# A two-layer decoder trunk in float32 on one core: both feed-forward stages with twelve up-projection pairs as seven block products each, the weight sums added by GpSimd in SBUF

## The chip, the core and the metric

The kernel runs on one core of a Trainium2 chip. The engines of a core are TensorE (PE in the profile; its weight loads are PEld), VectorE (DVE), ScalarE (ACT), GpSimd (POOL) and SyncE (SP, which issues most DMAs). They have separate instruction queues, each worked in order, and wait for each other by semaphores. The metric is the device time of one execution in microseconds (us), lower is better. The kernel before takes 1279.8 us, the median of 3 runs (1279.74 to 1279.89).

## The reference

Two layers, each a mixer (attention, a convolution module and a short gated convolution over one input projection) and a feed-forward network (FFN), on 16 + 512 = 528 tokens of width 1024. The change concerns the FFN:

```python
D_MODEL, DEPTH, D_FF, FFN_KERNEL = 1024, 2, 2816, 3

def ffn_sublayer(h, pre_g, post_g, w_up, conv_w, w_down):
    u = rms_norm(h, pre_g)
    z = jnp.einsum("bld,df->blf", u, w_up)
    z = causal_depthwise_conv(z, conv_w)
    g, up = jnp.split(z, 2, axis=-1)
    y = jnp.einsum("blf,fd->bld", jax.nn.silu(g) * up, w_down)
    return h + rms_norm(y, post_g)
```

In the last layer only 514 tokens are computed in the up projection and 512 behind it, since the first 16 are dropped.

## The kernel before

**Layout.** Activations lie transposed: 128 partitions are 128 of the 1024 features, the free dimension is the tokens. The 2816 FFN features are 22 chunks of 128. For a chunk f there is a pair of weight chunks, gate (columns 128 f) and up (columns 2816 + 128 f), each 1024 by 128, in SBUF [128, 8 x 128]. The 22 pairs are taken in three parts (`PARTS`: 8, 7 and 7), and after each part its share of the down projection is made and added to `yp`.

**Precision.** Each float32 operand is split into `hi`, rounded to the fast matmul type, and `lo`, the rest. A product is three matmuls: hi·hi, w-hi·u-lo and w-lo·u-hi. For a weight chunk ScalarE makes `whi` (a CAST) and VectorE `wlo` (a subtraction). An ordinary pair is 2 chunks x 8 rows of blocks x 3 x 2 halves of the tokens = 96 matmuls of 264 (layer 0) or 264 and 250 columns (layer 1), in `mm3`.

**Seven products.** In layer 1 only (`SEVEN_IN`), for the twelve pairs in `SEVEN`, the pair is one two-by-two block product: the gate and up chunks, each with an upper and a lower half of the 1024 rows, against two halves of the rows and of the tokens of u. `seven_pair` makes it from seven block products of 4 x 3 = 12 matmuls, 84 in all, of 258 columns, in three PSUM banks x, y and z. The inputs are sums of blocks. Those of u are made once per FFN by `normalised` (tiles t0 to t3, on ScalarE and VectorE, during part 0). Those of the weights, with gate0, gate1, up0, up1 for the halves, are gate0+up0, up0+up1, gate0+up0+up1 and gate0+gate1+up0+up1. A pair has four weight tiles, taken by `next_w` in this order: w (the gate chunk itself), c and b (two sums each) and d (up1 alone). The block sums leave more work to VectorE: 3.5 split chunks instead of 2, and additions behind PSUM.

**Where the sums come from.** `sum_steps` copies halves of the chunks to a DRAM tile `w_sum` with SP's DMAs and adds to them there with three accumulating DMAs of GpSimd's queue. `sums_at` spreads this: eight pairs during the FFN of layer 0, four in the mixer of layer 1. `tick` is a one-column GpSimd copy which ties each step to the progress of the FFN. In layer 1 the sums are loaded like weights.

**Order.** `next_w` keeps two weight tiles ready ahead of the one taken. Within an engine the order is fixed before the launch by a scheduler. `whi`/`wlo` have three buffers, shared by w, c and the down projection; `shi`/`slo` (for b) and the last pair of `y` (for d) have one. Raw weights rotate through three buffers, and in parts 1 and 2 of layer 1 through four more in the tile `h`, which is saved to `h_dram` for that time and loaded again (`spare`, `raw_tile`). `zs` (four buffers) holds up-projection outputs until `ffn_gate` has made the convolution (two SCALAR_TENSOR_TENSOR on VectorE for each of gate and up, behind one ACTIVATE), silu, product and split. In layer 0 the up projection reads the unscaled u, and `scaled` multiplies each output by `rz` on VectorE. `store_one` splits six chunks of layer 1's input projection in advance, in layer 0's down projections, and stores them by GpSimd's DMA (`w_split`).

Of the kernel before, what the change touches and what calls it, by code (L numbers as in the profile page):

```python
# [10 lines left out]
F32 = mybir.dt.float32  # L11
# [5 lines left out]
P = 128  # L17
# [11 lines left out]
PARTS = (8, 7, 7)  # L29


SEVEN = (8, 9, 10, 11, 12, 13, 15, 16, 17, 18, 19, 20)
SEVEN_IN = (1,)
SUMS = {1: (8, 4)}
SUM_US, SUM_LAT, SUM_EVERY = 0.9, 5.0, 40.0
K2 = KD // 2
SB = K2 * P
AHEAD = 2
# [350 lines left out]
def tile_hybrid_trunk(ctx: ExitStack, tc: tile.TileContext, xT, wflat, pv_d, out):  # L389
# [79 lines left out]
    nc.gpsimd.memset(hsel[DH:, DH:], 1.0 / DH)  # L469

    cols = T(const, [P, 4], F32, "cols")
    ticks = cols[:, 3:]
# [41 lines left out]


    up_chunk = {(c[1], c[4][0][0] // P): i for i, c in enumerate(chunks) if c[0] == "ffn_w_up"}
    seven_up = {up_chunk[l, NF + f]: (l, f) for l in SEVEN_IN for f in SEVEN}
    sums = {}

    def flat_w(i):  # L520

        n = chunks[i][3] * chunk_cols(chunks[i])
        return wflat[offs[i]:offs[i] + P * n].rearrange("(p s) -> p s", p=P)

    def sum_steps(l, f):

        gate, up = (flat_w(up_chunk[l, t]) for t in (f, NF + f))
        t = sums[l, f] = T(dram, [P, 4, SB], F32, f"w_sum{l}_{f}")
        n, o = P * 2 * SB, offs[up_chunk[l, f]]
        diag = wflat[o:o + 2 * (n + SB)].rearrange("(e q) -> e q", e=2)[:, :n].rearrange("e (p s) -> p e s", p=P)[:, :, :SB]  # L530

        def put(to, src):
            nc.gpsimd.dma_start(to, src, accum_op=ALU.add)

        def copies():
            with tc.issue_after(last_load[0].ins):
                nc.sync.dma_start(t[:, 0], up[:, :SB])
                nc.sync.dma_start(t[:, 1], up[:, :SB])
                nc.sync.dma_start(t[:, 2:4], gate.rearrange("p (e s) -> p e s", e=2))

        return copies, lambda: put(t[:, 0:2], diag), lambda: put(t[:, 2], t[:, 1]), lambda: put(t[:, 3], t[:, 2])

    def sums_at(l, place):

        counts = SUMS.get(l, ())
        n0 = sum(counts[:place])
        return SEVEN[n0:n0 + counts[place]] if place < len(counts) else ()

    pw_place = [None]

# [8 lines left out]
    parts, last_load = deque(), [None]  # L559
    spare, n_raw = [None], [0]  # L560

    def raw_tile():

        if spare[0] is not None:
            n_raw[0] += 1
            j = (None, 0, None, 1, None, 2, 3)[n_raw[0] % 7]
            if j is not None:
                return spare[0][:, 2 * j:2 * j + 2, :].rearrange("p a b -> p (a b)")
        return T(wp, [P, CHUNK], F32, "raw", 3)

    def prep_one():
        i = wpos[0]
        if i >= len(chunks):
            return
        if i in seven_up:
            if not parts:
                t = sums[seven_up[i]]
                parts.extend((("c", t[:, 1::2]), ("b", t[:, 0:3:2]), ("d", flat_w(i)[:, SB:])))
            kind, src = parts.popleft()
            wpos[0] += not parts  # L580
            raw = raw_tile()
            sz = SB if kind == "d" else 2 * SB
            nc.sync.dma_start(raw[:, :sz] if kind == "d" else raw[:, :sz].rearrange("p (e s) -> p e s", e=2),
                              src)
# [6 lines left out]
            nc.scalar.copy(hi[:, :sz], raw[:, :sz])  # L591
            nc.vector.tensor_sub(lo[:, :sz], raw[:, :sz], hi[:, :sz].bitcast(F32))
# [5 lines left out]
        raw = raw_tile()  # L598
        last_load[0] = nc.sync.dma_start(raw[:, :sz], wflat[offs[i]:offs[i] + P * sz].rearrange("(p s) -> p s", p=P))
        hi, lo = wtile(i, "whi"), wtile(i, "wlo")  # L600
        nc.scalar.copy(hi[:, :sz], raw[:, :sz])  # L601
        nc.vector.tensor_sub(lo[:, :sz], raw[:, :sz], hi[:, :sz].bitcast(F32))  # L602
        ready.append((i, tuple(t[:, :sz].rearrange("p (k n) -> p k n", n=n) for t in (hi, lo))))
# [6 lines left out]
    def store_one():  # L610

        if fetched:
            i, sz, raw = fetched.popleft()
            hi, lo = (T(wx[0], [P, WCHUNK], F32R, t) if sz <= WCHUNK else T(wp, [P, CHUNK], F32R, t) for t in ("whi", "wlo"))
            nc.scalar.copy(hi[:, :sz], raw[:, :sz])
            nc.vector.tensor_sub(lo[:, :sz], raw[:, :sz], hi[:, :sz].bitcast(F32))
            stored[i] = T(dram, [P, 2, sz], F32, f"w_split{i}")
            for n, t in enumerate((hi, lo)):
                nc.gpsimd.dma_start(stored[i][:, n], t[:, :sz].bitcast(F32))
        if to_store:  # L620
            i = to_store.popleft()
            sz = chunks[i][3] * chunk_cols(chunks[i])
            raw = T(wp, [P, CHUNK], F32, "raw", 3)
# [10 lines left out]
    def next_w():  # L634
        prefetch(1 + AHEAD)
        return ready.popleft()[1]
# [7 lines left out]
    def gp(us, fn, *after, **kw):  # L644
        return flow.op("pool", us, fn, after, **kw)
# [428 lines left out]
    def mixer(l, ypool, first, close_first, spans, front, rzs, u_at):  # L1074
# [720 lines left out]
        for i, f in enumerate(sums_at(l, 1)):  # L1795
            copies, *adds = sum_steps(l, f)
            tok = flow.op("sp", 2.0, copies, (Tok(flow.pe + SUM_EVERY * i),), prio=8, lat=SUM_LAT)
            for op in adds:
                tok = gp(SUM_US, op, tok, prio=8, lat=SUM_LAT)
# [243 lines left out]
    for l in range(DEPTH):  # L2043
# [23 lines left out]
        with tc.tile_pool(name=f"fp{l}", bufs=2, reuse_waits="tile") as fp:  # L2067
# [81 lines left out]
            def tick(src):  # L2149

                if todo:
                    t = nc.gpsimd.tensor_copy(ticks, src.bitcast(F32))
                    with tc.issue_after(t.ins):
                        todo.popleft()()

            def normalised():

                pools.pop().close()
# [79 lines left out]
            def seven_pair(f):  # L2238
# [13 lines left out]
                def t(i):  # L2252
                    return lambda b, k: ts[i][b][:, k, :]
# [36 lines left out]
            f0 = 0  # L2290
            for part, nf in enumerate(PARTS):
                for f in range(f0, f0 + nf):
                    if g:
                        tick(g[max(g)][0][:, :1])
                    if f in seven:
                        seven_pair(f)
                        if f == seven[-1]:
# [33 lines left out]
                if part < len(PARTS) - 1:  # L2331
                    for some in ((0, 1), *((m,) for m in range(2, KD))):
# [24 lines left out]
                else:  # L2357
                    assert not todo and building[0] is None
# [73 lines left out]
```

## Time and profile before

| | |
|---|---|
| median of 3 runs | 1279.8 us |
| profiled execution | 1280.6 us, of which 1278.7 us is the span of its instructions |
| HBM read, written | 151.09 MB, 37.95 MB |
| FFN of layer 0 | about 240 to 640 us of the span |
| FFN of layer 1 | about 880 to 1265 us; its seven products 1040 to 1108 and 1152 to 1220 us |

"x" is a count of instructions. Matmuls overlap, so TensorE's progress is read from how many start in a stretch and not from the duration of one. A row of the timeline is: start, duration of the merged instructions, engine, line, operation, output<-inputs, shape, count, and in brackets the idle time before it with what ended it.

### The profile page before, as it was taken

How to read it: one execution, taken by the hardware profiler on the slowest of the kernel's cores; microseconds unless marked ns; L12 is line 12 of the kernel's file. 1: busy time of each engine (PE TensorE's matmuls, PEld its weight loads, DVE VectorE, ACT ScalarE, POOL GpSimd, SP SyncE). 2: the span in 40 equal slices, each digit the busy share in tenths (PEclk: the TensorE clock that was granted, in tenths of full speed). 3: DMA queues.
4: the chain of work that ended last, by engine and by line, in shares of the span. 5: the costliest groups of instructions: out<-in, count | busy, mean ns of one | idle time of the engine just before them, and what ended most of it. 6: DMA issues, size and time to landing. Idle time of an engine off the chain costs nothing.

```text
span 1278.7 us, 24208 instructions
## 1 busy us (share of the span) xinstructions
PE 1259.6 (99%) x9660; PEld 1208.0 (94%) x9660; DVE 888.4 (69%) x1505; ACT 667.0 (52%) x1273; POOL 154.7 (12%) x333
## 2 busy tenths in 40 slices
PE   8999999999999999999999999999999999999997
PEld 8999899999999999999999998989999789979997
DVE  7888765688733774466587878765799738746964
ACT  7254577564333442233573546766554447626753
POOL 1313311001122112100003234120000000000000
PEclk9999999999999999999999999999999999999999
DMA  7136132705579647832461675536234235434611
GB/s 242 34 102 160 51 101 76 234 25 149 138 235 264 158 106 229 215 92 89 145 248 50 168 174 129 140 80 220 85 97 152 94 118 166 151 116 151 203 63 66
DMA packets 69393, 176.30 MB, mean 138 GB/s; under 512 B 7632, under 2 KB 18000, under 8 KB 69024
## 3 DMA queue, kind: packets, MB, share of 16 engines
q1 hardware_dynamic: 60784, 155.74, 38.4%
q0 software_dynamic: 8496, 19.01, 8.5%
q8 instruction: 76, 1.25, 0.4%
q14 instruction: 37, 0.30, 0.1%
HBM read 151.09 MB, written 37.95 MB: 148 GB/s over the span
## 4 chain that ended last, share of the span: by engine, by line
PE 93%; DVE 3%; ACT 1%; DMA 1%; issue 1%; POOL 0%; SPq 0%; DVEq 0%; ACTq 0%
PE psum L786 69%; PE psum L2234 9%; PE psum L1356 4%; PE psum L1620 3%; PE psum L1586 2%; PE psum L923 1%; PE psum L1542 1%; PE psum L1686 1%; PE psum L1272 1%; DMA raw<-in_w_dram 0%; DVE yp L999 0%; POOL dm L1557 0%; DMA h<-in_x_dram 0%; ACT whi L738 0%; DVE h L1009 0%
## 5 line engine op out<-in xcount | busy, mean ns | idle before, releaser
L786 PE MATMUL psum<-y,whi 128*128 128x264 f32 (+3 forms) x1968 | 384.1, 299 | 3.2 <-ACT yp L2351 1.7
L786 PE MATMUL psum<-uhi,whi 128*128 128x264 f32 (+1 forms) x1456 | 349.8, 288 | 2.7 <-DVE zs L2085 0.9
L786 PE MATMUL psum<-ulo,whi 128*128 128x264 f32 (+1 forms) x1456 | 343.4, 284 | 0.6 <-DVE ulo L2020 0.4
L786 PE MATMUL psum<-uhi,wlo 128*128 128x264 f32 (+1 forms) x1456 | 342.4, 284 | 0.0
L786 PEld LDWEIGHTS psum<-y,whi 128*128 128x128 f32 x1968 | 304.7, 188 | 17.5 <-ACT yp L2351 2.3
L786 PE MATMUL psum<-y,wlo 128*128 128x264 f32 (+3 forms) x984 | 272.7, 297 | 0.3 <-DVE wlo L742 0.3
L786 PEld LDWEIGHTS psum<-uhi,whi 128*128 128x128 f32 x1456 | 245.9, 188 | 7.4 <-issue 2.0
L786 PEld LDWEIGHTS psum<-ulo,whi 128*128 128x128 f32 x1456 | 246.0, 188 | 1.3 <-DVE ulo L2020 0.6
L786 PEld LDWEIGHTS psum<-uhi,wlo 128*128 128x128 f32 x1456 | 245.6, 188 | 0.0
L786 PEld LDWEIGHTS psum<-y,wlo 128*128 128x128 f32 x984 | 177.1, 188 | 5.7 <-DVE wlo L742 0.6
L601 ACT CAST whi<-raw 128x1024 fp32r<-128x1024 f32 (+1 forms) x80 | 82.2, 1029 | 114.4 <-PE psum L786 85.0
L2122 DVE SCALAR_TENSOR_TENSOR c<-zs,pv,c 128x528 f32<-128x528 f32 (+1 forms) x176 | 131.2, 757 | 11.2 <-ACT c L2120 9.2
L602 DVE TENSOR_TENSOR wlo<-raw,whi 128x1024 fp32r<-128x1024 f32 (+1 forms) x80 | 95.8, 1198 | 43.5 <-ACT whi L601 42.7
L742 DVE TENSOR_TENSOR wlo<-raw,whi 128x1024 fp32r<-128x1024 f32 (+2 forms) x80 | 95.6, 1204 | 29.8 <-ACT whi L738 29.3
L738 ACT CAST whi<-raw 128x1024 fp32r<-128x1024 f32 (+2 forms) x80 | 81.7, 1030 | 26.9 <-PE psum L786 20.0
L1102 DVE SCALAR_TENSOR_TENSOR cacc<-apad,pv,cacc 128x528 f32<-128x528 f32 x120 | 87.6, 772 | 0.1
L2120 ACT ACTIVATE c<-zs,pv 128x528 f32<-128x528 f32 (+1 forms) x88 | 63.2, 727 | 4.1 <-DVE zs L2272 1.5
L2136 ACT CAST y<-c 128x528 fp32r<-128x528 f32 (+1 forms) x44 | 27.6, 627 | 71.2 <-DVE c L2133 71.2
L2085 DVE TENSOR_TENSOR zs<-psum,rz 128x528 f32<-128x528 f32 x40 | 28.3, 707 | 47.7 <-PE psum L786 46.9
L1620 PE MATMUL psum<-pf,vals 128*128 128x400 f32 (+3 forms) x160 | 50.7, 399 | 0.6 <-POOL pf L1600 0.6
L1586 PE MATMUL psum<-q,k 128*128 128x128 f32 (+2 forms) x192 | 51.1, 348 | 0.0
L2132 ACT ACTIVATE c<-c 128x528 f32<-128x528 f32 (+1 forms) x44 | 28.1, 640 | 43.8 <-DVE c L2122 43.8
(265 smaller groups left out, 1972.5 us busy)
## 6 DMA issues: line engine op xcount, KB each, us to landing
raw<-in_w_dram SPq DMA_DIRECT2D x135, 512.0 KB, 4.3
raw<-in_w_dram SPq DMA_DIRECT2D x27, 448.0 KB, 4.4
h<-w_sum SPq DMA_DIRECT2D x14, 512.0 KB, 4.2
h<-in_w_dram SPq DMA_DIRECT2D x13, 512.0 KB, 3.8
w_sum<-in_w_dram SPq DMA_DIRECT2D x24, 256.0 KB, 8.5
w_sum<-in_w_dram SPq DMA_DIRECT2D x12, 512.0 KB, 7.3
w_sum<-in_w_dram POOLq DMA_DIRECT2D x12, 512.0 KB, 7.3
w_sum<-w_sum POOLq DMA_DIRECT2D x24, 256.0 KB, 5.6
```

What stands on the lines that cost most here:

```text
L601: nc.scalar.copy(hi[:, :sz], raw[:, :sz])
L602: nc.vector.tensor_sub(lo[:, :sz], raw[:, :sz], hi[:, :sz].bitcast(F32))
L738: nc.scalar.copy(box["hi"][:, :sz], box["raw"][:, :sz])
L742: nc.vector.tensor_sub(lo[:, :sz], box["raw"][:, :sz], box["hi"][:, :sz].bitcast(F32))
L786: nc.tensor.matmul(d, lhsT=w[a][:, k, cols], rhs=rhs(b, k, hf), start=start and i == 0 and p == 0, stop=stop and i == n - 1 and p == 2)
L1102: nc.vector.scalar_tensor_tensor(conv[j], in0=src, in1=conv[j], scalar=col("a_dw_w", CK * j + i), op0=ALU.mult, op1=ALU.add)
L1356: nc.tensor.matmul(ps[:n, :nw], lhsT=(uhi, ulo)[ui][:, k, P * b:P * b + n], rhs=w[wi][:, k % 4, :], start=k == 0 and p == 0, stop=k == KD ...
L1586: nc.tensor.matmul(s, lhsT=k[:, ka:ka + kn], rhs=q[:, s0:qz], start=i == 0, stop=i == 1)
L1620: nc.tensor.matmul(acc[:, s0 - qa:qz - qa], lhsT=vals[:, b].rearrange("p h d -> p (h d)")[:, o:o + P], rhs=box["p"], start=b == 0, stop=b ...
L2120: nc.scalar.activation(dst, src[:, 2:2 + 2 * fw], AF.Copy, scale=wtap(2, t))
L2122: nc.vector.scalar_tensor_tensor(dst, in0=src[:, i:i + 2 * fw], scalar=wtap(i, t), in1=dst, op0=ALU.mult, op1=ALU.add)
L2234: nc.tensor.matmul(psum[:, bank, :n7], lhsT=w[a][:, k0 + k, :], rhs=rhs(b, k), start=start and k == 0 and p == 0, stop=stop and k == K2 - ...
```

## The change

The seven products are now used in both layers for the same twelve pairs (f = 8 to 13 and 15 to 20), so layer 0 too builds t0 to t3, saves and reloads `h`, and evacuates its parts 1 and 2 on ScalarE (`zs` copies) instead of `scaled`. In layer 0 the products have 264 columns.

`w_sum`, `sum_steps`, `sums_at` and `tick` are gone. When the first sum of a pair is wanted, `prep_one` loads the up chunk into a raw tile, takes a third raw tile `more`, and has GpSimd make the sums by four additions of [128, 512] float32 in SBUF: up0+up1 and gate0+up0+up1 into `more` (c), then gate1+gate0+up0+up1 and gate0+up0 over the gate chunk (b). The last two overwrite the gate chunk, so they wait until ScalarE and VectorE have split it. The second halves of b and c have changed places, so b is taken two products later than before.

`store_one` now runs only in the down projection of part 1, once for each of its eight outputs, and uses the `shi`/`slo` tiles.

```diff
-SEVEN = (8, 9, 10, 11, 12, 13, 15, 16, 17, 18, 19, 20)
-SEVEN_IN = (1,)
-SUMS = {1: (8, 4)}
-SUM_US, SUM_LAT, SUM_EVERY = 0.9, 5.0, 40.0
+SEVEN = DEPTH * ((8, 9, 10, 11, 12, 13, 15, 16, 17, 18, 19, 20),)
...
-    def sum_steps(l, f):
-
-        gate, up = (flat_w(up_chunk[l, t]) for t in (f, NF + f))
-        t = sums[l, f] = T(dram, [P, 4, SB], F32, f"w_sum{l}_{f}")
...
-        def put(to, src):
-            nc.gpsimd.dma_start(to, src, accum_op=ALU.add)
...
-        return copies, lambda: put(t[:, 0:2], diag), lambda: put(t[:, 2], t[:, 1]), lambda: put(t[:, 3], t[:, 2])
...
         if i in seven_up:
             if not parts:
-                t = sums[seven_up[i]]
-                parts.extend((("c", t[:, 1::2]), ("b", t[:, 0:3:2]), ("d", flat_w(i)[:, SB:])))
-            kind, src = parts.popleft()
+                gate, up, more = last_raw[0], raw_tile(), raw_tile()
+                x, y = slice(0, SB), slice(SB, 2 * SB)
+                last_load[0] = nc.sync.dma_start(up[:, :2 * SB], flat_w(i))
+                for to, p, q in ((more[:, x], up[:, x], up[:, y]), (more[:, y], gate[:, x], more[:, x]),
+                                 (gate[:, y], gate[:, y], more[:, y]), (gate[:, x], gate[:, x], up[:, x])):
+                    nc.gpsimd.tensor_add(to, p, q)
+                parts.extend((("c", more), ("b", gate), ("d", up[:, y])))
+            kind, raw = parts.popleft()
             wpos[0] += not parts
-            raw = raw_tile()
...
-            hi, lo = (T(wx[0], [P, WCHUNK], F32R, t) if sz <= WCHUNK else T(wp, [P, CHUNK], F32R, t) for t in ("whi", "wlo"))
+            hi, lo = (T(tx[0], [P, 2 * SB], F32R, t) for t in ("shi", "slo")) if sz <= 2 * SB else (T(wp, [P, CHUNK], F32R, t) for t in ("whi", "wlo"))
...
-            seven = SEVEN if l in SEVEN_IN else ()
-            todo = deque(step for to, place in ((l + 1, 0), (l, 2)) for f in sums_at(to, place) for step in sum_steps(to, f))
...
+            seven = SEVEN[l]
...
                 finish_pair()
-                wb = next_w()
-                product(y, wb, K2, t(1), False, False)
+                product(y, wc, K2, t(1), False, False)
                 nc.scalar.copy(gate[:, hi], by[:, skip:])
                 product(x, w, K2, u(K2, h7[0]), False, True)
                 nc.scalar.copy(gate[:, lo], bx)
-                product(z, wc, K2, u(K2, h7[1]), False, True)
+                wb = next_w()
+                product(z, wb, K2, u(K2, h7[1]), False, True)
...
-                            if l == 0 and m % 2:
-                                store_one()
-                            tick(yp[:, m, t0:t0 + 1])
+                        if l == 0 and part == 1:
+                            store_one()
```

On GpSimd, in layer 0 from the end of part 0 on, there were ticks and accumulating DMAs:

```order
L2152 COPY cols_103<-y_430_4062 128x1
L533 DMA w_sum_9_385_3532<-in_w_dram 128x2x512
L2152 COPY cols_103<-y_439_4187 128x1
L533 DMA w_sum_9_385_3532<-w_sum_9_385_3532 128x512
L619 DMA w_split_464_4549<-whi_4545 128x1024
L619 DMA w_split_464_4549<-wlo_4546 128x1024
```

Now the additions of the pairs f = 9 and 10 stand there (the `h` rows are raw tiles in `h`):

```order
L557 TENSOR_TENSOR raw_4856<-raw_4856,raw_4889 128x512
L557 TENSOR_TENSOR raw_4856<-raw_4856,h_2820 128x512
L557 TENSOR_TENSOR raw_5018<-h_2820 128x512
L557 TENSOR_TENSOR raw_5018<-h_2820,raw_5018 128x512
L557 TENSOR_TENSOR h_2820<-h_2820,raw_5018 128x512
L557 TENSOR_TENSOR h_2820<-h_2820 128x512
```

The last two of pair 9 (raw_4856 is its gate chunk) stand ahead of the first two of pair 10 (raw_5018 is its `more`), so these wait behind the split of the gate chunk of pair 9.

On VectorE, in part 1 of layer 0, one pair was two weight splits, two scalings, four convolution steps, a product and a split:

```order
L2085 TENSOR_TENSOR zs_2813<-psum_67,rz_2811 128x528
L602 TENSOR_TENSOR wlo_5116<-raw_5113,whi_5115 128x1024
L2122 SCALAR_TENSOR_TENSOR c_5168<-zs_2813,pv_3_69,c_5168 128x528 x2
L2085 TENSOR_TENSOR zs_2813<-psum_67,rz_2811 128x528
L602 TENSOR_TENSOR wlo_5186<-raw_5183,whi_5185 128x1024
L2122 SCALAR_TENSOR_TENSOR c_5172<-zs_2813,pv_3_69,c_5172 128x528 x2
L2133 TENSOR_TENSOR c_5168<-c_5168,c_5172 128x528
L2140 TENSOR_TENSOR y_512_5178<-c_5168,y_512_5178 128x528
```

Now (around pairs 11 and 12; L579 is w, L569 with `wlo` is c, with `slo` b, with `y` d):

```order
L569 TENSOR_TENSOR wlo_5153<-h_2820,whi_5152 128x1024
L579 TENSOR_TENSOR wlo_5245<-raw_5242,whi_5244 128x1024
L569 TENSOR_TENSOR y_497_5045<-h_2820,y_497_5045 128x512
L2234 TENSOR_TENSOR zs_2813<-psum_67,zs_2813 128x264
L2093 SCALAR_TENSOR_TENSOR c_5079<-zs_2813,pv_3_69,c_5079 128x528
L2093 SCALAR_TENSOR_TENSOR c_5203<-zs_2813,pv_3_69,c_5203 128x528
L2093 SCALAR_TENSOR_TENSOR c_5079<-zs_2813,pv_3_69,c_5079 128x528
L2093 SCALAR_TENSOR_TENSOR c_5203<-zs_2813,pv_3_69,c_5203 128x528
L569 TENSOR_TENSOR slo_5157<-h_2820,shi_5156 128x1024
L2237 TENSOR_TENSOR zs_2813<-zs_2813,acc_5060 128x264
L2104 TENSOR_TENSOR c_5075<-c_5075,c_5079 128x528
L569 TENSOR_TENSOR y_509_5173<-raw_5146,y_509_5173 128x512
```

The split of b for pair 11 (slo_5157) stands behind four convolution steps, and nearly every row here reads two operands from SBUF.

More of the change, by code (lines that the diff above doesn't have):

```diff
@@ L471, in tile_hybrid_trunk @@
     cols = T(const, [P, 4], F32, "cols")
-    ticks = cols[:, 3:]
     for i, val in enumerate((1.0, RMS_EPS, LN_EPS)):
@@ L516, in tile_hybrid_trunk @@
     up_chunk = {(c[1], c[4][0][0] // P): i for i, c in enumerate(chunks) if c[0] == "ffn_w_up"}
-    seven_up = {up_chunk[l, NF + f]: (l, f) for l in SEVEN_IN for f in SEVEN}
-    sums = {}
+    seven_up = {up_chunk[l, NF + f]: (l, f) for l in range(DEPTH) for f in SEVEN[l]}
     def flat_w(i):
@@ L523, in flat_w @@
         return wflat[offs[i]:offs[i] + P * n].rearrange("(p s) -> p s", p=P)
-    def sum_steps(l, f):
-        gate, up = (flat_w(up_chunk[l, t]) for t in (f, NF + f))
-        t = sums[l, f] = T(dram, [P, 4, SB], F32, f"w_sum{l}_{f}")
-        n, o = P * 2 * SB, offs[up_chunk[l, f]]
-        diag = wflat[o:o + 2 * (n + SB)].rearrange("(e q) -> e q", e=2)[:, :n].rearrange("e (p s) -> p e s", p=P)[:, :, :SB]
-        def put(to, src):
[L533 to L539, printed above, removed]
-        return copies, lambda: put(t[:, 0:2], diag), lambda: put(t[:, 2], t[:, 1]), lambda: put(t[:, 3], t[:, 2])
[L543 to L547, printed above, removed]
     pw_place = [None]
@@ L557, in wtile, with spare_tile @@
         return T(wx[0], [P, WCHUNK], F32R, tag) if i in wide else T(wp, [P, CHUNK], F32R, tag)
-    parts, last_load = deque(), [None]
+    parts, last_load, last_raw = deque(), [None], [None]
     spare, n_raw = [None], [0]
+    def spare_tile(j):
+        return spare[0][:, 2 * j:2 * j + 2, :].rearrange("p a b -> p (a b)")
     def raw_tile():
         if spare[0] is not None:
+            j = (None, 0, None, 1, None, 2, 3)[n_raw[0] % 7]
             n_raw[0] += 1
-            j = (None, 0, None, 1, None, 2, 3)[n_raw[0] % 7]
             if j is not None:
-                return spare[0][:, 2 * j:2 * j + 2, :].rearrange("p a b -> p (a b)")
+                return spare_tile(j)
         return T(wp, [P, CHUNK], F32, "raw", 3)
@@ L576, in prep_one @@
             if not parts:
-                t = sums[seven_up[i]]
-                parts.extend((("c", t[:, 1::2]), ("b", t[:, 0:3:2]), ("d", flat_w(i)[:, SB:])))
-            kind, src = parts.popleft()
+                gate, up, more = last_raw[0], raw_tile(), raw_tile()
[6 more added lines that the diff above has]
+            kind, raw = parts.popleft()
             wpos[0] += not parts
-            raw = raw_tile()
             sz = SB if kind == "d" else 2 * SB
-            nc.sync.dma_start(raw[:, :sz] if kind == "d" else raw[:, :sz].rearrange("p (e s) -> p e s", e=2),
-                              src)
             if kind == "b":
@@ L597, in prep_one @@
         sz = kn * n
-        raw = raw_tile()
+        raw = last_raw[0] = raw_tile()
         last_load[0] = nc.sync.dma_start(raw[:, :sz], wflat[offs[i]:offs[i] + P * sz].rearrange("(p s) -> p s", p=P))
@@ L622, in store_one @@
             sz = chunks[i][3] * chunk_cols(chunks[i])
-            raw = T(wp, [P, CHUNK], F32, "raw", 3)
+            raw = raw_tile()
             nc.sync.dma_start(raw[:, :sz], wflat[offs[i]:offs[i] + P * sz].rearrange("(p s) -> p s", p=P))
@@ L1793, in then @@
                 early.begin(1, PAIRS[1], *banks["st"].slots)
[L1795 to L1799, printed above, removed]
         for g in (then("maxima", maxima()), att_norms(), then("exponentials", exponentials()), then("fill", fill())):
@@ L2145, in tile_hybrid_trunk @@
             late_ups = deque()
-            seven = SEVEN if l in SEVEN_IN else ()
-            todo = deque(step for to, place in ((l + 1, 0), (l, 2)) for f in sums_at(to, place) for step in sum_steps(to, f))
[L2149 to L2154, printed above, removed]
+            seven = SEVEN[l]
             def normalised():
@@ L2292, in tile_hybrid_trunk @@
                 for f in range(f0, f0 + nf):
-                    if g:
-                        tick(g[max(g)][0][:, :1])
                     if f in seven:
@@ L2353, in tile_hybrid_trunk @@
                                 nc.vector.tensor_add(d, d, src)
-                            if l == 0 and m % 2:
-                                store_one()
-                            tick(yp[:, m, t0:t0 + 1])
+                        if l == 0 and part == 1:
+                            store_one()
                 else:
-                    assert not todo and building[0] is None
+                    assert building[0] is None
                     if seven:
```

## The prediction

> **What bounds the kernel now.** First the page: the span, the busy shares and the chain that ended last.
>
> ```profile
> span 1278.7 us, 24208 instructions
> PE 1259.6 (99%) x9660; PEld 1208.0 (94%) x9660; DVE 888.4 (69%) x1505; ACT 667.0 (52%) x1273; POOL 154.7 (12%) x333
> PE 93%; DVE 3%; ACT 1%; DMA 1%; issue 1%; POOL 0%; SPq 0%; DVEq 0%; ACTq 0%
> PE psum L786 69%; PE psum L2234 9%; PE psum L1356 4%; PE psum L1620 3%; PE psum L1586 2%; PE psum L923 1%; PE psum L1542 1%; PE psum L1686 1%; PE psum L1272 1%; DMA raw<-in_w_dram 0%; DVE yp L999 0%; POOL dm L1557 0%; DMA h<-in_x_dram 0%; ACT whi L738 0%; DVE h L1009 0%
> ```
>
> TensorE is the chain: every matmul taken away counts, as long as its operands are there in time. The same windows give the price of a matmul and the room on the other engines, in layer 0's part 0 (second row) and in layer 1's stretches of seven products.
>
> ```profile
> core 0: us, PE busy (x) PEld busy (x) DVE busy (x) ACT busy (x) POOL busy (x), PEclk, DMA share, GB/s
> 280.00:320.00 40.00, 40.00 (x329) 40.00 (x329) 31.28 (x42) 20.79 (x27) 6.31 (x7) 1.00 0.51 133
> 1160.00:1200.00 40.00, 40.00 (x335) 40.00 (x334) 32.80 (x44) 29.15 (x52) 0.00 (x0) 1.00 0.51 154
> 1045.00:1100.00 55.00, 55.00 (x460) 55.00 (x459) 44.39 (x59) 41.00 (x73) 0.00 (x0) 1.00 0.56 180
> 1156.00:1210.00 54.00, 54.00 (x452) 54.00 (x451) 43.34 (x57) 39.22 (x70) 0.00 (x0) 1.00 0.54 171
> ```
>
> A matmul of 264 columns costs 40.00/329 = 121.6 ns, one of layer 1's mix (mostly 258 columns) 119.4. TensorE waits for nothing there, the clock is full, and VectorE is 80.5% busy (44.39 of 55, 43.34 of 54). GpSimd does nothing in these stretches. That is what changes.
>
> **The matmuls saved.** Twelve pairs of layer 0 go from 96 to 84 matmuls, and two that prime the banks are added: 142 fewer. At 121.6 ns that is 17.3 us. The columns of the seven products stay 264; scaled from layer 1's 258 (6 columns at the 2.5 ns that 329 against 335 suggests, so some 123 ns) a pair is 84 x 0.123 = 10.3 us instead of 11.7, 16.1 us for twelve. I take **-16.7 us**.
>
> **Layer 0's part 0.** Layer 0 now builds t0 to t3 as layer 1 does. Layer 1's windows price this: part 0 there, then the same of layer 0 (240 to 280 and 320 to 400; 280 to 320 stands above).
>
> ```profile
> 880.00:920.00 40.00, 39.10 (x315) 38.18 (x314) 31.14 (x56) 23.32 (x48) 0.00 (x0) 1.00 0.36 127
> 920.00:960.00 40.00, 39.80 (x329) 39.50 (x329) 32.54 (x57) 19.90 (x28) 0.00 (x0) 1.00 0.27 80
> 960.00:1000.00 40.00, 40.00 (x313) 38.92 (x312) 36.45 (x60) 18.71 (x27) 0.00 (x0) 1.00 0.46 144
> 1000.00:1040.00 40.00, 39.03 (x169) 31.21 (x169) 18.72 (x19) 16.66 (x23) 0.00 (x0) 1.00 0.27 93
> 240.00:280.00 40.00, 40.00 (x318) 39.47 (x317) 32.65 (x59) 23.33 (x49) 0.00 (x0) 1.00 0.25 81
> 320.00:360.00 40.00, 40.00 (x331) 40.00 (x329) 26.68 (x33) 14.91 (x19) 4.99 (x7) 1.00 0.54 140
> 360.00:400.00 40.00, 39.30 (x325) 39.09 (x324) 13.80 (x13) 14.31 (x18) 10.60 (x18) 1.00 0.88 261
> ```
>
> TensorE stands 0.90 + 0.20 + 0 + 0.97 = 2.1 us in layer 1, 0.7 us in layer 0. So **+1.4 us**, between 0 and 2.1.
>
> **The additions on GpSimd.** No GpSimd instruction with two tensors is in this trace, so its price is bounded by the ones that read SBUF. What matters more is what they do to VectorE. First GpSimd alone, then beside VectorE's two-operand steps (L1102 reads apad and cacc from SBUF):
>
> ```profile
> 775.17 0.29 POOL L1600 TENSOR_SCALAR_AFFINE_SELECT pf<-pf 128x128 f32<-128x128 f32 x1
> 775.65 0.37 POOL L1557 TENSOR_SCALAR dm<-ident,mcol 128x128 fp32r<-128x128 f32 x1 [0.18 <-DVE mcol L1549]
> 779.00 0.21 POOL L1600 TENSOR_SCALAR_AFFINE_SELECT p<-p 16x16 f32<-16x16 f32 x1 [0.41 <-ACT p L1593]
> 776.89 2.95 DVE L1102 SCALAR_TENSOR_TENSOR cacc<-apad,pv,cacc 128x528 f32<-128x528 f32 x4
> 777.07 0.82 POOL L1557 TENSOR_SCALAR dm<-ident,mcol 128x128 fp32r<-128x128 f32 x1
> 777.85 0.75 POOL L1600 TENSOR_SCALAR_AFFINE_SELECT pf<-pf 128x128 f32<-128x128 f32 x1
> 789.73 2.12 DVE L1102 SCALAR_TENSOR_TENSOR cacc<-apad,pv,cacc 128x528 f32<-128x528 f32 x3
> L1102 DVE SCALAR_TENSOR_TENSOR cacc<-apad,pv,cacc x120: 745/762/937, 45.0 to 801.9; 128x528 f32<-128x528 f32 x120
> ```
>
> Three steps alone take 2.12 us, so one more costs (2.12 - 0.76)/2 = 0.68 and four should take 2.80. They took 2.95. Meanwhile the two GpSimd instructions took 0.82 and 0.75 instead of 0.37 and 0.29. The first ends at 777.89, 0.24 us behind the end of the first step (776.89 + 0.76); the second, by the same count, 0.15 behind the next one. So **GpSimd's read waits until VectorE's step has ended, and VectorE's next step is put off in turn**: 0.24 + 0.15 less two hand-overs of 0.12 is the 0.15 lost. They take turns; the reads do not overlap.
>
> An addition reads 512 elements from two inputs. The nearest row is dm, which has two inputs: 0.24 for 128 gives 4 x 0.24 = 0.96, less 0.12: **VectorE loses 0.8 us per contested addition**. Low end: one input at pf's slope, (0.29 - 0.21)/112 = 0.7 ns, 0.05 + 0.36 - 0.12, about 0.3. High end: no free hand-over and dm's start on top, 0.96 + 0.24 = 1.2. Below nothing it cannot go: a neighbour that takes turns never speeds VectorE up.
>
> [...]
>
> How many are contested? VectorE idles 19.5% of a pair of 10.1 us: 2.0 us. Four additions lose 3.2. But of the 24 additions of a part's six pairs, ten (pairs 1 and 2, half of pair 3) fall into the down projection ahead or into the first 7 us, when VectorE has to wait for weight buffers to come free. The other 14 meet 3.5 pairs with 6.9 us of idle, and there is a lead: a c block's buffer comes free 36 matmuls (4.4 us) ahead of its use, and its two splits need these:
>
> ```profile
> L601 ACT CAST whi<-raw 128x1024 fp32r<-128x1024 f32 x65 | 68.2, 1049 | 98.8 <-PE psum L786 76.4 <-issue 12.7 <-DMA raw<-in_w_dram 8.7
> L602 DVE TENSOR_TENSOR wlo<-raw,whi 128x1024 fp32r<-128x1024 f32 x65 | 79.5, 1223 | 39.8 <-ACT whi L601 39.3
> L592 DVE TENSOR_TENSOR y<-raw,y 128x512 fp32r<-128x512 f32 x6 | 4.1, 688 | 3.8 <-ACT y L591 3.8
> L2085 DVE TENSOR_TENSOR zs<-psum,rz 128x528 f32<-128x528 f32 x40 | 28.3, 707 | 47.7 <-PE psum L786 46.9
> ```
>
> 1.05 + 1.22 = 2.3 leaves 2.1. So a part comes out late by 14 x 0.8 - 6.9 - 2.1 = 2.2 us, first at the c and b blocks of pairs 4 to 6, and four parts (two in each layer) by **+8.8 us**. Layer 1 pays too, though it saves nothing.
>
> Layer 0's extra splits (1.22 + 0.69 per pair) stand against scalings that go (28 x 0.707 = 20 us), so VectorE's 80.5% of layer 1 holds for layer 0 too; its slightly longer rows I take as nothing, since its pairs are longer as well.
>
> **What costs nothing.** These end or start in the shadow of TensorE:
>
> ```profile
> L533 POOL DMA_DIRECT2D w_sum<-w_sum x24 | 20.2, 840 | 78.4 <-DMA w_sum<-in_w_dram 44.8 <-DMA w_sum<-w_sum 33.1 <-issue 0.5
> raw<-in_w_dram SPq DMA_DIRECT2D x135, 512.0 KB, 4.3
> w_sum<-in_w_dram POOLq DMA_DIRECT2D x12, 512.0 KB, 7.3
> h_dram<-h SPq DMA_DIRECT2D x2, 1056.0 KB
> h<-h_dram SPq DMA_DIRECT2D x4, 528.0 KB, 3.6
> ```
>
> The 36 accumulating DMAs, 36 copies on SP and 32 ticks that go: no wait of TensorE in the chain names them. The up chunk's load (4.3 us) is issued more than a pair (10 us) ahead, with seven raw tiles for three per pair; without that cover every pair would wait 4.3 us. The second halves of b and c: b is wanted 24 matmuls (2.9 us) later, which is already in the lead above. `h` saved and loaded in layer 0 (four loads of 3.6 us) has pair 21 and a down projection of some 40 us ahead of its use; if that were short, 4 us once. `store_one`'s six chunks (2.3 us each) and their GpSimd DMAs move into one down projection, where VectorE has room; GpSimd's additions for pair 15 stand among them, 12 DMAs at 0.84 us late at worst, with 40 us to do it.
>
> **Sum.** 1280.6 (profiled execution: span 1278.7 and 1.9 around it) - 16.7 + 1.4 + 8.8 = 1274.1; the median of the runs shown lies 0.8 lower: **1273.3 us**, I say 1273.5, -0.5%.
>
> **Rivals.** (1) *The additions fit into VectorE's idle time* (loss 0.6 or less: 14 x 0.6 = 8.4 is under 6.9 + 2.1): 1279.8 - 15.3 = 1264.5. For it: 10 us of idle VectorE per part. Against: the idle time is waiting in a fixed order and cannot be filled at will. (2) *VectorE becomes the bound in all four parts, and the change loses.* At a loss of 1.05 a part is 14.7 - 9.0 = 5.7 us late, 23 in all: 1279.8 - 15.3 + 23 = 1287.5. It decides from 0.91 on, where 14 x 0.91 - 9.0 = 3.8 per part eats the 15.3. For it: the high end, 1.2 (7.8 per part, 1295.7), and ScalarE, whose casts stand behind steps that wait for VectorE. Against: dm's row. (3) *GpSimd itself is late*: the sums of a pair stand behind the split of the gate chunk ahead, so c waits for GpSimd. At 1.0 us (0.96 and a start) and half a VectorE step (0.5) of waiting, four additions need 6 of 10.3 us, so unlikely; with 1 us per pair it gives 24 - 15.3, 1288.5. That the matmuls don't go is no rival: their number in the program is fixed.
>
> **Numbers.** The forecast 0.42 (1269 to 1279), rival 1 0.20, rival 2 0.32, rival 3 0.06. The range leaves out half of rival 1's lower side and the upper part of rival 2: 1263.5 to 1292. A measurement can tell 0.2%, 2.6 us. Faster by more: 0.35 of the forecast and rival 1, 0.55; within: 0.07 and 0.04 of rival 2, 0.11; slower: the rest of rival 2 and rival 3, 0.34.
>
> **What would show it.** GpSimd's TENSOR_TENSOR rows: near 1.0 us alone, up to 2 us beside VectorE. VectorE's splits and convolution steps longer than 1.22 and 0.75 in the four parts, its busy share near 95%. TensorE idle before L2196 (the seven products) released by VectorE's `wlo`/`slo` in pairs 4 to 6: 2 us per part says the forecast, none rival 1, 5 rival 2; released by GpSimd or by casts waiting for it, rival 3. Layer 0's part 0 with 2 us of idle TensorE. It is wrong if layer 1 costs the same as before, or if the losses lie elsewhere, say at the reload of `h`.

## The result, and the profile after

The changed kernel takes **1297.0 us** (median of four runs, 1294.1 to 1299.4) against 1279.9 before: a ratio of 1.0132, 95% interval 1.011 to 1.0154. The forecast was 1273.5 us with a range up to 1292: wrong in sign, and the time lies above the range. The profiled execution took 1296.1 us. Its page, first the span, the busy shares and the chain that ended last:

```profile
span 1294.4 us, 24062 instructions
...
PE 1253.1 (97%) x9518; PEld 1198.5 (93%) x9518; DVE 976.6 (75%) x1561; ACT 713.5 (55%) x1389; POOL 255.7 (20%) x361
...
PE 46%; DVE 7%; issue 2%; ACT 2%; POOL 1%; DMA 1%; DVEq 0%; ACTq 0%; POOLq 0%
```

The 142 matmuls are gone (x9518 against x9660), yet the span is 15.7 us longer. The profile follows the chain back only to 526 us, so its shares add up to 59% and not to the 99% of before; in that stretch VectorE, ScalarE and GpSimd hold 10 of the 59, where they held 4 of the 99. The lines meant below are those of the changed kernel: L557 the additions, L568 and L569 the cast and the subtraction that split c, b and d (L578 and L579 those of w), L2093 a convolution step, L2196 the seven products. The view of TensorE's waits gives the sum in us, the count and the longest:

```profile
PE psum L2196 <- DVE slo L569: 10.3, 8, 2.4
PE psum L2196 <- ACT whi L568: 9.1, 4, 3.8
```

Neither row exists before. TensorE waits 10.3 us for VectorE's half of b's split and 9.1 us for ScalarE's cast of c. The next view, busy time by windows (with the columns of the windows in the prediction), shows a stretch with layer 1's part 1 and one with layer 0's part 2, first after, then before:

```profile
1005.00:1110.00 105.00, 98.85 (x661) 91.65 (x660) 81.91 (x83) 58.34 (x100) 38.46 (x24) 0.97 0.30 94
500.00:585.00 85.00, 80.65 (x620) 79.67 (x619) 65.91 (x63) 43.60 (x72) 40.23 (x30) 0.94 0.39 129
```

```profile
1005.00:1110.00 105.00, 104.03 (x728) 96.94 (x726) 69.34 (x87) 65.66 (x110) 0.00 (x0) 1.00 0.45 146
500.00:585.00 85.00, 85.00 (x699) 85.00 (x699) 48.95 (x58) 29.01 (x36) 10.54 (x17) 1.00 0.59 162
```

In layer 1 VectorE is busy for 12.6 us more with four instructions fewer (81.91, x83, against 69.34, x87), and TensorE starts 67 matmuls fewer. In both stretches the granted clock is below 1.00, which it was not before. How VectorE gets longer is seen in a few rows of the timeline (start, duration of the merged instructions); VectorE first, then GpSimd:

```profile
1061.87 3.34 DVE L2093 SCALAR_TENSOR_TENSOR c<-zs,pv,c 128x512 f32<-128x512 f32 x2
1065.13 2.31 DVE L569 TENSOR_TENSOR slo<-raw,shi 128x1024 fp32r<-128x1024 f32 x1
...
1061.35 1.61 POOL L557 TENSOR_TENSOR h<-h,raw 128x512 f32<-128x512 f32 x1 [1.23 <-DVE wlo L579]
1062.93 1.73 POOL L557 TENSOR_TENSOR h<-h 128x512 f32<-128x512 f32 x1
1064.62 1.73 POOL L557 TENSOR_TENSOR h<-raw 128x512 f32<-128x512 f32 x1
```

Three additions meet three VectorE steps in turn. Two convolution steps take 3.34 us; two at 1090.37, with no addition beside them, take 1.53. The third addition ends at 1066.35, 1.14 us behind the end of the second step (1061.87 + 3.34 = 1065.21), and the split behind it takes 2.31 us instead of 1.22: **1.09 us lost to one addition**.

Two groups of VectorE steps of one size show which steps lose. The first reads one operand from PSUM (the banks that TensorE writes) and one from SBUF, the second both from SBUF (smallest, median and largest duration in ns):

```profile
L2234 DVE TENSOR_TENSOR zs<-psum,zs x24: 409/420/427, 409.8 to 1226.2; 128x264 f32<-128x264 f32 x12, 128x256 f32<-128x256 f32 x12
L2237 DVE TENSOR_TENSOR zs<-zs,acc x24: 409/420/1512, 415.8 to 1228.9; 128x264 f32<-128x264 f32 x12, 128x256 f32<-128x256 f32 x12
```

In the timeline 13 steps of the first group run beside an addition, and none is longer than 0.43 us. Of the second group two run beside one, and they take 1.51 us instead of 0.42.

How this reaches TensorE, at the longest stall of layer 1 (rows of VectorE, GpSimd, ScalarE and TensorE in the same view; the bracket is the idle time before a row and what ended it):

```profile
1086.09 2.32 DVE L569 TENSOR_TENSOR slo<-h,shi 128x1024 fp32r<-128x1024 f32 x1
1088.33 1.51 DVE L2237 TENSOR_TENSOR zs<-zs,acc 128x256 f32<-128x256 f32 x1
1089.76 0.68 DVE L2104 TENSOR_TENSOR c<-c,c 128x512 f32<-128x512 f32 x1
...
1085.70 3.86 POOL L557 TENSOR_TENSOR raw<-raw,h 128x512 f32<-128x512 f32 x2
...
1090.48 0.62 ACT L2107 CAST y<-c 128x512 fp32r<-128x512 f32 x1 [6.01 <-DVE c L2104]
...
1093.07 1.03 ACT L568 CAST whi<-h 128x1024 fp32r<-128x1024 f32 x1
...
1094.16 0.80 PE L2196 MATMUL psum<-t,whi 128*128 128x258 f32 x2 [3.83 <-ACT whi L568]
```

VectorE's split and a zs step (1.51 instead of 0.41) have each lost 1.1 us beside two additions. ScalarE stands 6.01 us behind the product on VectorE, with the cast of the next c five places behind in its fixed order; when it comes, TensorE has waited 3.83 us. And then TensorE starts again at a lower granted clock (third column from the end): these are windows around four of the stalls, the last of them wholly behind its stall and at 0.50.

```profile
524.00:531.00 7.00, 5.13 (x30) 4.96 (x30) 3.55 (x3) 2.03 (x4) 4.75 (x4) 0.76 0.36 123
565.00:575.00 10.00, 7.84 (x39) 7.33 (x38) 9.39 (x12) 7.18 (x13) 3.28 (x2) 0.66 0.16 52
1211.00:1220.00 9.00, 5.42 (x32) 5.21 (x31) 8.82 (x13) 7.75 (x14) 0.00 (x0) 0.81 0.64 214
1094.00:1100.00 6.00, 5.84 (x27) 5.85 (x28) 6.00 (x9) 4.43 (x9) 0.00 (x0) 0.50 0.66 197
```

Between 1094 and 1100 TensorE waits for next to nothing and starts 27 matmuls in 6 us, 0.22 us each instead of 0.12. The starts of the matmuls in the trace show 82 such in the four places, each 0.0975 us above the usual: 82 x 0.0975 = **8 us lost to the clock**.

### The profile page after: what moved, and what is told of

It is laid out like the page before. It is cut to its first block, busy times and chain, and to the rows that moved or that the text cites. A ratio compares the mean times of both kernels' runs of the same rounds, so it can differ in the third digit from the quotient of the medians.

```text
span 1294.4 us, 24062 instructions
## 1 busy us (share of the span) xinstructions
PE 1253.1 (97%) x9518; PEld 1198.5 (93%) x9518; DVE 976.6 (75%) x1561; ACT 713.5 (55%) x1389; POOL 255.7 (20%) x361
## 4 chain that ended last, share of the span: by engine, by line
PE 46%; DVE 7%; issue 2%; ACT 2%; POOL 1%; DMA 1%; DVEq 0%; ACTq 0%; POOLq 0%
PE psum L763 33%; PE psum L2196 6%; DVE c L2093 2%; PE psum L1333 2%; PE psum L1597 2%; PE psum L900 1%; DVE slo L569 1%; PE psum L1563 1%; DVE wlo L579 1%; DMA h<-in_w_dram 1%; POOL raw L557 1%; PE psum L1519 0%; ACT whi L578 0%; ACT c L2091 0%; DVE yp L976 0%
## 5 line engine op out<-in xcount | busy, mean ns | idle before, releaser
L763 PE MATMUL psum<-uhi,whi 128*128 128x264 f32 (+1 forms) x1072 | 271.4, 289 | 1.5 <-ACT uhi L1989 0.7
L763 PE MATMUL psum<-ulo,whi 128*128 128x264 f32 (+1 forms) x1072 | 265.5, 284 | 0.6 <-DVE ulo L1991 0.4
L763 PE MATMUL psum<-uhi,wlo 128*128 128x264 f32 (+1 forms) x1072 | 264.5, 283 | 0.0
L763 PEld LDWEIGHTS psum<-uhi,whi 128*128 128x128 f32 x1072 | 186.5, 189 | 5.9 <-issue 1.6
L763 PEld LDWEIGHTS psum<-ulo,whi 128*128 128x128 f32 x1072 | 186.6, 189 | 1.3 <-DVE ulo L1991 0.6
L763 PEld LDWEIGHTS psum<-uhi,wlo 128*128 128x128 f32 x1072 | 186.0, 188 | 0.0
L2093 DVE SCALAR_TENSOR_TENSOR c<-zs,pv,c 128x528 f32<-128x528 f32 (+1 forms) x176 | 162.8, 942 | 13.1 <-ACT c L2091 11.3
L578 ACT CAST whi<-raw 128x1024 fp32r<-128x1024 f32 (+1 forms) x53 | 54.4, 1027 | 68.3 <-PE psum L763 47.7
L557 POOL TENSOR_TENSOR h<-raw 128x512 f32<-128x512 f32 x11 | 17.1, 1556 | 368.9 <-DVE wlo L579 363.1
L2196 PE MATMUL psum<-t,whi 128*128 128x264 f32 (+1 forms) x384 | 75.1, 292 | 10.9 <-ACT whi L568 9.1
L579 DVE TENSOR_TENSOR wlo<-raw,whi 128x1024 fp32r<-128x1024 f32 (+1 forms) x53 | 67.7, 1278 | 13.3 <-ACT whi L578 12.9
L2196 PEld LDWEIGHTS psum<-t,whi 128*128 128x128 f32 x384 | 61.6, 195 | 12.3 <-ACT whi L568 10.0
L579 DVE TENSOR_TENSOR wlo<-h,whi 128x1024 fp32r<-128x1024 f32 (+1 forms) x33 | 43.1, 1310 | 29.1 <-ACT whi L578 29.0
```

The lines of the kernel that those rows point to most:

```text
L557: nc.gpsimd.tensor_add(to, p, q)
L763: nc.tensor.matmul(d, lhsT=w[a][:, k, cols], rhs=rhs(b, k, hf), start=start and i == 0 and p == 0, stop=stop and i == n - 1 and p == 2)
L2093: nc.vector.scalar_tensor_tensor(dst, in0=src[:, i:i + 2 * fw], scalar=wtap(i, t), in1=dst, op0=ALU.mult, op1=ALU.add)
L2196: nc.tensor.matmul(psum[:, bank, :n7], lhsT=w[a][:, k0 + k, :], rhs=rhs(b, k), start=start and k == 0 and p == 0, stop=stop and k == K2 - ...
```

## The experiments

Three theories. A: an addition on GpSimd takes about 1.1 us from VectorE whenever it meets a VectorE step with two operands in SBUF; splits, and the casts queued behind VectorE's results, come late, and the stalls pull the clock down. B: layer 0's own new work is at fault (18 more split chunks, evacuations on ScalarE, `store_one` in one place). C: GpSimd itself is too slow, its sums being in the chain.

**1. Without the additions.**

```diff
-                for to, p, q in (...):
-                    nc.gpsimd.tensor_add(to, p, q)
-                parts.extend((("c", more), ("b", gate), ("d", up[:, y])))
+                parts.extend((("c", up), ("b", gate), ("d", up[:, y])))
```

> The 96 additions are left out: c is split from the up chunk and b from the gate chunk as loaded, so the block sums are missing from the result; loads, splits, casts, products and evacuations stay. Theory A (each addition beside VectorE's two-operand steps takes about 1.1 us from VectorE, splits and the casts queued behind them come late, and the long stalls lower TensorE's clock): 1279.9 - 16.7 + 0.5 = 1263.7, between 1262 and 1267, granted clock 0.999, no stall of TensorE over 1 us in the pairs of seven products. Theory B (layer 0's own extra work is at fault: 18 more split chunks, evacuations moved to ScalarE, store_one in one place): above 1275. Theory C (GpSimd itself is late, its sums come behind the split of the gate chunk ahead): 1264 here as well; the next run parts it from A.

Measured: 1264.2 us, ratio 0.9872 (0.9858 to 0.9887), granted clock of the profiled run 0.998. The additions cost 33 us and all else that the change brought into layer 0 costs nothing that shows: B falls.

**2. Writes in place of additions.**

```diff
-                    nc.gpsimd.tensor_add(to, p, q)
+                    nc.gpsimd.memset(to, 0.01)
```

> Each addition is replaced by a GpSimd memset of the same 128x512 tile (the sums are constants then): same number of GpSimd instructions in the same places, the same buffers written, the split of b still behind the overwriting of the gate chunk, but GpSimd reads nothing. Theory A: VectorE's splits and convolution steps are back at 1.22 and 0.75 us, and the time is 1262 to 1268 with the clock at 0.998 or more. Theory C: as GpSimd is still in the chain, b and c stay late; if a memset takes near the 1.3 us of an addition, about 1290, if it takes a third, some 1272.

Measured: 1262.5 us, 0.9857 (0.9842 to 0.9872), clock 0.999. The page, then one group of VectorE's splits (smallest, median and largest duration in ns) here and in the changed kernel:

```profile
span 1261.1 us, 24044 instructions
...
PE 1241.7 (98%) x9518; PEld 1190.2 (94%) x9518; DVE 915.2 (73%) x1561; ACT 717.6 (57%) x1389; POOL 150.9 (12%) x361
```

```profile
L569 DVE TENSOR_TENSOR slo<-raw,shi x10: 1217/1220/1227, 411.7 to 1186.7; 128x1024 fp32r<-128x1024 f32 x10
```

```profile
L569 DVE TENSOR_TENSOR slo<-raw,shi x10: 1212/2284/2316, 413.5 to 1219.6; 128x1024 fp32r<-128x1024 f32 x10
```

With the same 1561 instructions VectorE is busy 915.2 us instead of 976.6: **61.4 us come from the 96 additions**. The split is at 1.22 us in all ten cases, where it had a median of 2.28. The memsets, which only write, did not lengthen VectorE's splits.

**3. Writes as long as the additions.** A memset takes 0.53 us, an addition 1.58 on the mean (GpSimd is busy 255.7 us with the additions and 103.8 without them, over 96), so C was not yet excluded.

```diff
-                    nc.gpsimd.tensor_add(to, p, q)
+                    for _ in range(3):
+                        nc.gpsimd.memset(to, 0.01)
```

> Three memsets of 128x512 in place of each addition: GpSimd is then busy for 3 x 0.53 = 1.58 us per sum, as long as the 1.60 us that an addition took on the mean in the changed kernel, but reads nothing (the sums are constants). Theory A: as with one memset, 1261 to 1266, VectorE's steps not longer. Theory C (GpSimd's own time makes b and c late): 1285 or more.

Measured: 1262.7 us, 0.9861 (0.9841 to 0.9881). GpSimd is busy 241.2 us, nearly as long as with the additions, at the same places of its queue, and none of TensorE's waits is on b's or c's splits: C falls.

**4. One operand instead of two.**

```diff
-                    nc.gpsimd.tensor_add(to, p, q)
+                    nc.gpsimd.tensor_copy(to, p if p is not to else q)
```

> Each addition is replaced by a GpSimd copy of its first operand (one SBUF input instead of two; the sums are missing from the result). If what VectorE loses goes by the elements that GpSimd reads: a copy takes about 0.7 us alone and costs a contested step some 0.5 us, so 14 x 0.5 - 9.0 is below nothing and the time is 1262 to 1267. If any reading GpSimd instruction costs a VectorE step the same 1.1 us, whatever it reads, the time stays at 1290 to 1299.

Measured: 1262.3 us, 0.986 (0.9845 to 0.9876), clock 0.999. Two meetings in the timeline, VectorE's rows, then GpSimd's, and below them the same group of splits as above:

```profile
1044.26 1.84 DVE L2093 SCALAR_TENSOR_TENSOR c<-zs,pv,c 128x512 f32<-128x512 f32 x2 [0.19 <-ACT c L2091]
1046.02 1.62 DVE L569 TENSOR_TENSOR slo<-raw,shi 128x1024 fp32r<-128x1024 f32 x1
...
1045.51 1.06 POOL L557 COPY h<-raw 128x512 f32<-128x512 f32 x1
```

```profile
L569 DVE TENSOR_TENSOR slo<-raw,shi x10: 1215/1624/1630, 411.6 to 1185.7; 128x1024 fp32r<-128x1024 f32 x10
```

Beside a copy, which reads one tile, the split loses 0.40 us (1.62 against 1.22), beside an addition, which reads two, 1.09. Whether it is the size of what GpSimd reads or the time it reads for was not parted. VectorE is busy for 929.3 us in this run, 14.1 more than with memsets: 3.5 us per part, under the 9.0 of idle time and lead, and TensorE notices nothing.

**5. Half the dose.** c's two sums by additions, b's two as memsets.

```diff
-                                 (gate[:, y], gate[:, y], more[:, y]), (gate[:, x], gate[:, x], up[:, x])):
-                    nc.gpsimd.tensor_add(to, p, q)
+                nc.gpsimd.memset(gate[:, y], 0.01)
+                nc.gpsimd.memset(gate[:, x], 0.01)
```

> Half of the dose: the two sums of c are added on GpSimd, the two of b are GpSimd memsets (constants instead of sums, so the result differs there). Theory A with a threshold: 7 contested additions x 1.08 = 7.6 us per part is under the 9.0 of idle time and lead, so nearly nothing is left: 1263 to 1268, clock 0.998. If each contested addition costs TensorE its share without a threshold (33.5 us over 96 additions), half of it stays: about 1279.

Measured: 1266.6 us, 0.9889 (0.9875 to 0.9904). VectorE is busy for 944.3 us, 29.1 more than with memsets, about half of the 61.4. Yet half of the additions cost 4 us over the run with memsets, all of them 34: there is a threshold, as the prediction's formula has it. No run has b's additions alone, so it is open whether b's two weigh as much as c's.

**6. Layer 1 alone.**

```diff
-SEVEN = DEPTH * ((8, 9, 10, 11, 12, 13, 15, 16, 17, 18, 19, 20),)
+SEVEN = ((), (8, 9, 10, 11, 12, 13, 15, 16, 17, 18, 19, 20))
...
-                        if l == 0 and part == 1:
-                            store_one()
+                            if l == 0 and m % 2:
+                                store_one()
```

(`store_one`, its tiles included, is as in the kernel before.)

> Seven products in layer 1 only, as before the change, with the sums made by GpSimd in SBUF as after it; layer 0 as before (96 matmuls per pair, store_one spread). The additions are then all that differs from before. Theory A: layer 1 loses the 13 us that its excess over TensorE's usual pace shows (30.3 us against 17.1): 1290 to 1295, clock 0.994 to 0.997. Theory B: within 2 us of before, 1278 to 1282. My forecast's 2.2 us per part would give 1284.

Measured: 1294.3 us, 1.0106 (1.0091 to 1.0121), clock 0.997. With the same matmuls as before the change, sums on GpSimd in place of sums in DRAM cost 13 us, 6.4 for each of layer 1's two parts, where the forecast had 2.2. TensorE's two new waits (the lines of L568 and L569, as above) are 10.4 of it, 5.2 per part; 30 matmuls at half rate are 3 more.

**7. Sums in DRAM for both layers**, on the kernel before:

```diff
-SEVEN_IN = (1,)
-SUMS = {1: (8, 4)}
+SEVEN_IN = (0, 1)
+SUMS = {0: (0, 12), 1: (8, 4)}
...
-            tok = flow.op("sp", 2.0, copies, (Tok(flow.pe + SUM_EVERY * i),), prio=8, lat=SUM_LAT)
+            tok = flow.op("sp", 2.0, copies, (Tok(flow.pe + SUM_EVERY[l] * i),), prio=8, lat=SUM_LAT)
```

(`SUM_EVERY` is 15 us for layer 0; `store_one` as in the changed kernel.)

> Seven products in both layers with the sums made in DRAM by accumulating DMAs as before: layer 0's twelve in the mixer ahead of it, 15 us apart, layer 1's as they were. Theory A: the whole gain of the 142 matmuls, 1262 to 1268, unless the 36 more accumulating DMAs disturb the mixer of layer 0. Theory B: above 1275. If the sums of layer 0 come too late, TensorE waits for the DMA of raw in part 1 of layer 0.

Measured: 1305.1 us, 1.0207 (1.0175 to 1.0239). A miss for A as put there: the additions are gone, but not the cost. One window over the mixer of layer 0, for this kernel and for the run with memsets:

```profile
60.00:240.00 180.00, 162.49 (x1154) 146.87 (x1153) 119.17 (x283) 96.03 (x247) 60.43 (x116) 0.97 0.89 199
```

```profile
60.00:240.00 180.00, 178.72 (x1339) 164.77 (x1339) 130.34 (x297) 110.73 (x272) 35.58 (x89) 1.00 0.38 112
```

Layer 0's sums sit in the mixer, where the DMA share goes from 0.38 to 0.89, GpSimd from 35.6 to 60.4 us, and TensorE starts 185 matmuls fewer. So the place is bad; whether the memory traffic or GpSimd's 36 DMA issues among the mixer's own steps do the harm was not taken apart (among TensorE's longest waits are 8.3 us for GpSimd's `pf` and 3.6 for a DMA of `k`). Nor is the mixer all of it: from 500 to 585 us, in layer 0's FFN, where sums for layer 1 are made, the DMA share is 0.88 against 0.45 with memsets, and TensorE starts 604 matmuls against 694. That sums in DRAM are cheap in layer 1 doesn't carry over.

**8. The additions on VectorE.**

```diff
-                    nc.gpsimd.tensor_add(to, p, q)
+                    nc.vector.tensor_add(to, p, q)
```

> The same four additions per pair on VectorE instead of GpSimd. By theory A a contested addition of GpSimd takes 1.08 us from VectorE; one of its own of 128x512 should take 0.69 (the split of d, same size, takes 0.685). By the count of the prediction a part is then late by 14 x 0.69 - 9.0 = 0.7 us, 2.6 in all over the 1262.5 of the run with memsets: 1265, between 1263 and 1275, clock 0.997 or more. If what matters is only that the sums are made late or in a chain, moving them changes little: 1290.

Measured: 1269.9 us, 0.9912 (0.9895 to 0.9928). The same additions on the engine that they starved are 27 us faster than on the idle one. It stays 7 us above the run with memsets; the longest new wait stands behind layer 0's additions to `yp`:

```profile
PE psum L2196 <- DVE yp L2313: 3.3, 1, 3.3
```

**9. Early additions on GpSimd, late ones on VectorE.**

```diff
-                    nc.gpsimd.tensor_add(to, p, q)
+                    (nc.gpsimd if seven_up[i][1] in (8, 9, 10, 15, 16, 17) else nc.vector).tensor_add(to, p, q)
```

> The first three pairs of each part have their additions on GpSimd (they are made during the down projection or in the first pair, where VectorE has room), the last three on VectorE. Theory A: no worse than with all on VectorE, 1263 to 1270; less VectorE work ahead of the part, so perhaps 1 us better. If the early additions did harm too, it lies between that run and the changed kernel.

Measured: **1267.7 us, 0.9903 (0.9888 to 0.9918)**: 1.0% below the kernel before and the fastest of the kernels that make all sums, though its interval overlaps that of the run before it. Additions that fall where VectorE has room did little harm here.

**10. The same with `store_one` spread** over the down projections of parts 0 and 1. By the order of the loads, the chunk loaded at the end of part 0 is here overwritten in `h` before it is split in part 1, so one chunk of layer 1's input projection holds other values; the work is the same.

```diff
-                        if l == 0 and part == 1:
-                            store_one()
+                            if l == 0 and m % 2:
+                                store_one()
```

> The mixed kernel (first three pairs' additions on GpSimd, last three on VectorE) with store_one spread over the down projections of parts 0 and 1 of layer 0, every second output as before the change, instead of once for each output of part 1. What is left over the run with memsets (1267.7 against 1262.5) stands partly at layer 0's part 1: stalls of 1.95 and 1.56 us behind the additions to yp and a slow stretch of the clock of 3.3 us. If store_one in one place is the cause: these go, 1263 to 1266. If they come from the additions themselves or from the down projection as such: within 1 us of 1267.7.

Measured: 1271.5 us, 0.9924 (0.9911 to 0.9938). Slower by 4 us, so spreading `store_one` is no gain. What keeps the mixed kernel above 1262.5 stays open.

## Why the prediction was wrong, step by step

**The step that failed: "VectorE loses 0.8 us per contested addition".** It came from `dm`, "which has two inputs"; but `dm` reads one 128x128 tensor and a column, not two tensors. The copies show one full input of 512 at 0.40 us, the additions two at 1.09. So four times `dm`'s 0.24 was too much for one input and was not doubled for the second; that 0.8 came as near as it did is luck. Put into the prediction's own formula, 14 x 1.09 - 6.9 - 2.1 = 6.3 us per part and 25 in all, where 8.8 stood. The changed kernel and the run with memsets issue the same 9518 matmuls in the same order, so their starts can be compared one by one: stalls add 25.7 us, 4.3 to 6.6 in the pairs of each part. This is what rival 2 said (1287.5 at 1.05, its high end 1.2; no row of before shows the 1.05, and the runs showed 1.09); it had a chance of 0.32. The bounds, 0.3 to 1.2, did hold the value; the choice inside them was wrong, with a row that seemed near and was not.

An addition alone was put at near 1.0 us. The shortest, which has no VectorE step beside it, took 1.28 (first of the three durations in ns):

```profile
L557 POOL TENSOR_TENSOR h<-h x29: 1278/1601/2163, 367.3 to 1203.7; 128x512 f32<-128x512 f32 x29
```

**The count of 14 exposed additions per part held.** Step by step against the run with memsets, 15, 14, 15 and 15 VectorE steps in the pairs of the four parts are longer by more than 0.15 us, by 13.6, 12.8, 14.3 and 13.9 us per part; most of the rest of the 61.4 us lies ahead of the pairs. So did the formula with its threshold (half the dose: 7 x 1.09 = 7.6, under 9.0, and 4 us lost instead of 34), the place (c and b of the late pairs) and that layer 1 pays too. The agreement of 25 with 25.7 is closer than the formula deserves: with the measured 12.8 to 14.3 in place of 14 x 1.09 it gives 18.6, so the 9.0 of idle time and lead was counted somewhat too high.

**A term was missing: the clock.** No step counted that TensorE came back at a granted clock of 0.50 behind four stalls of 2.0 to 4.0 us. That is 8 of the 33.3 us between the changed kernel's span and that of the memsets (1294.4 - 1261.1); the stalls are the rest, 19.4 of them in the two waits shown first. With the right price alone the prediction's sum is 1279.8 - 15.3 + 25 = 1289.5, inside its range; the clock's 8 us put the time above it.

**The matmuls saved and layer 0's part 0, -16.7 + 1.4 = -15.3**: with memsets the span fell by 17.6 us (1278.7 to 1261.1). 142 x 121.6 ns = 17.3 without the scaling to 264 columns was the better number, and the +1.4 for part 0 left no trace: at its end TensorE's starts are within 0.2 us of those before.

**"What costs nothing" held.** DMAs, copies, ticks, the load of the up chunk, b two products later, `h` saved and loaded and `store_one` are all in the run with memsets, and it has the whole gain.

Rival 1 (the additions fit into idle time) needed 0.6 per addition; it is what the copies do, at 0.40. Rival 3 (GpSimd late) was shown wrong by the three memsets.

## What to carry to other kernels

An idle engine is not always free room: here a GpSimd addition that met a VectorE split cost it 1.09 us, and an addition was cheaper on VectorE itself (0.69 us), although VectorE was 80% busy in the stretches of seven products of the kernel before. When a cost per instruction stands against a fixed amount of slack, the price at which it tips over matters more than the likeliest price; if the known bounds lie on both sides, say so in the chances. And a stall of TensorE is to be priced with what the clock does after it, here 8 of 33.3 us.

## What the runs showed of the hardware

- **VectorE beside GpSimd.** VectorE's split of 128x1024 (1.22 us) lost 1.09 us beside a GpSimd addition of 128x512, 0.40 beside a copy of that size, nothing beside a memset. Steps of 128x264 and 128x256 with one of their operands in PSUM lost nothing beside an addition (0.41 to 0.43 us, all 24, 13 of them beside one).
- **The clock came down behind some stalls, but not each one.** In the changed kernel stalls of 2.0, 2.0, 4.0 and 3.7 us (by the starts of the matmuls) were followed by 3 to 7 us of matmuls at 0.22 us instead of 0.12; the one of 2.58 us at 449.9 was not. What decides was not shown. The granted clock falls to 0.50 at 526.70, 567.66, 1093.31 and 1216.19 us, for 3.41, 6.83, 6.83 and 3.41 us, and at 1291.28, behind TensorE's last work, to the end of the span. The first four of these places lie 40.96, 525.65 and 122.88 us apart, that is 12, 154 and 36 times 3.413 us. These are a window with the greater part of the stall at 449.9, a window with the stall at 524.4, and the window behind that:

```profile
448.19:451.60 3.41, 1.96 (x17) 1.75 (x15) 3.41 (x3) 1.86 (x3) 3.25 (x2) 1.00 0.00 0
523.28:526.69 3.41, 1.54 (x13) 1.37 (x12) 2.23 (x3) 2.27 (x3) 2.63 (x3) 1.00 0.40 151
526.70:530.10 3.40, 3.40 (x17) 3.40 (x18) 1.31 (x1) 0.38 (x1) 2.24 (x3) 0.50 0.50 159
```

  In the window with the stall at 524.4 TensorE is busy for 1.54 us, in the one with the greater part of the longer stall at 449.9 for 1.96 us. No run moved a stall on purpose to test whether that is the difference. The changed kernel's runs spread by 0.4% (1294.1 to 1299.4, clock 0.988 to 0.992), the memsets' by 0.2%; where the spread comes from was not shown.
